# Stick-breaking attention handled two heads at a time, with split keys padded by zeros

## The chip, the cores and the metric

The kernel runs on one core of a Trainium2 chip, as one launch. The metric is the device time of that launch in microseconds; lower is better. The core has a matrix engine (TensorE, PE in the profile, with its weight loads as PEld), three engines for elementwise work (VectorE = DVE, ScalarE = ACT, GpSimd = POOL) and a queue for transfers (SyncE = SP). Each engine runs its own instructions in the order written and waits on the others through semaphores. Products of matrices end in PSUM banks of 128 x 512 float32.

## The reference

Two decoder blocks over 256 tokens of width 1024, in float32: first stick-breaking attention (12 heads of 64) beside softmax attention into 256 memory tokens, and a squared-relu feed-forward; then latent attention, a long convolution, and a convolutional feed-forward after each. The change touches the stick-breaking attention alone:

```
for blk in range(seq // 128):                       # two blocks of 128 queries
    t0 = blk * 128; t1 = t0 + 128
    z = einsum('bhtd,bhsd->bhts', q[t0:t1], k[:t1]) * 64 ** -0.5
    strict = arange(t1)[None, :] < arange(t0, t1)[:, None]
    log_stay = where(strict, log_sigmoid(-z), 0.0)
    later = cumsum(log_stay, axis=3, reverse=True) - log_stay
    w = where(strict, exp(log_sigmoid(z) + later), 0.0)
    out[t0:t1] = einsum('bhts,bhsd->bhtd', w, v[:t1])
```

So the weight of key s for query t is sigmoid(z[t, s]) times the product of sigmoid(-z[t, j]) over the keys j between s and t; keys at or after t count nothing.

## The kernel before

Every weight matrix comes from HBM in slabs of 128 x 1024 float32 (`weights`, L80). A slab is split into a high part on ACT (`whi`, L69) and a low part on DVE (`wlo`, L70), both in fp32r. A product is then three passes: high x high, low x high, high x low (`gemm_b`, `mm3`); the trace has one matmul record for such a pass and two for a product in plain float32. Raw slabs have a ring of 3 buffers, split ones a ring of 5, so SP can issue a slab's transfer only when the slab three places earlier has been split.

Stick-breaking attention comes second in the program, after the product for the values (`v_sb`). The 12 heads are 6 pairs, because one 128-row projection holds two heads of 64. `u_q(i)` and `u_k(i)` project the queries and keys of pair i: 24 matmuls of 256 columns each (L102) and one copy from PSUM on ACT (L351). The loop `pipeline` takes one head per turn: `scores` of the next head, then a filler (a projection for a later pair, or work of the memory attention), then `turn` of this head, then `values` of the head before.

- `scores` (L387 to L403) takes a head's 64 rows of q and k in plain float32: queries 0 to 127 against keys 0 to 128 (L391, 129 columns) and queries 128 to 255 against all keys (L393, 256 columns). After each, a bf16 product of the identity with a mask adds -1e30 where a key may not count (L392, L394). ACT takes sigmoid(-z/8) into `sb_stay` (L397) and sigmoid(z/8) into `sb_w` (L398), 385 columns each; DVE forms the running product from the right, `sb_later` (L400, a scan; `reset` starts it again at 1 between the two blocks), and multiplies `sb_w` by it (L402).
- `turn` transposes the weights on PE (L408, three 128 x 128 tiles into bank `wt`) and copies them back (L410).
- `values` multiplies by v in plain float32 (L418, L419) into half of the rows of bank `pv`; after the second head of a pair the result is split (`mix`).

The z banks of the two heads of a pair are two (`z00`, `z01`); the first sigmoid in the program needs another activation table (ACT_TABLE_LOAD).

The order on each engine is settled when the program is built: a scheduler places the instructions of these functions by its own model of their times.

Of the kernel before, what the change touches and what calls it, by code (L numbers as in the profile page):

```python
# [9 lines left out]
F32 = mybir.dt.float32  # L10
# [35 lines left out]
def block_kernel(ctx, tc, A, out, taps=None):  # L46
# [25 lines left out]
    # The splits of the slabs that follow a norm queue behind it on the vector engine.  # L72
# [7 lines left out]
    def weights(ap, dst=None):  # L80
        """Loads a slab of weights and splits it; where the vector engine is short, GpSimd shares the work."""
# [13 lines left out]
    def gemm_b(ps, w, off, x, kts):  # L95
        """ps[n, tok] = W[:, n-tile]^T x^T, x feature-major as (hi, lo)."""
# [29 lines left out]
    def range_reduce(dst, src, n, shift):  # L126
        """dst = src - 2 pi round(src / 2 pi + shift), kept inside the interval that Sin takes."""
# [50 lines left out]
    def first_mm(b, x, ws, utok):  # L178
        """The next product's first 512 columns for one token block, token-major."""
# [13 lines left out]
    def first_pair(utok, i, ps=None):  # L193
        """Two of the four first n-tiles, feature-major."""
# [55 lines left out]
    def spare(pool, tags):  # L250
        """Room outside the ring for the next product's first slabs: two of them for each pair of tags."""
# [45 lines left out]
    # ================= stick-breaking attention and memory attention =================  # L297
# [10 lines left out]
    # Products of zeros bring the tensor engine's clock up while the first loads are under way.  # L308
# [24 lines left out]
    identb = p1.tile([P, P], BF16, name="identb")  # L333
    nc.vector.tensor_copy(identb, ident)
    maskf = p1.tile([P, P + 1], F32, name="maskf")
    nc.sync.dma_start(maskf, A["c_mask"])
    maskb = p1.tile([P, P + 1], BF16, name="maskb")
    nc.vector.tensor_copy(maskb, maskf)
    reset = p1.tile([P, 385], F32, name="reset")
    nc.vector.memset(reset, 0.0)  # L340
    nc.vector.memset(reset[:, 128:129], 1.0)
    memx = (p1.tile([P, KT, S], F32R, name="mh"), p1.tile([P, KT, S], F32R, name="ml"))
# [10 lines left out]

    def u_q(i):
        proj(f"q_{i}", A["w_qk"][i], x, 3)

    def u_k(i):
        proj(f"k_{i}", A["w_qk"][6 + i], x, 3)
# [22 lines left out]
    class Stick:  # L381
        pv = None

        def __init__(self, head):
            self.h, self.pair, self.hh = head, head // 2, head % 2
# [26 lines left out]
        def values(self):  # L412
            if self.hh == 0:
                Stick.pv = acc_bank(1, 1, "pv")
# [764 lines left out]
```

## Time and profile before

| | us |
|---|---|
| median of three runs | 1000.65 (1000.11 to 1004.74) |
| span of the profiled execution | 1001.1 |
| PE busy in it | 963.8 (96%) |
| DVE, ACT, POOL busy | 752.7 (75%), 522.3 (52%), 123.5 (12%) |
| chain that ended last, share of PE | 76% |

The span runs from the first to the last instruction of one execution. PE counts as busy while a matmul is in it; matmuls overlap, so the time that one takes of a stream is read from starts, or from the chain of work that ended last, which follows the program back from its end and gives each piece only the time by which it held up the next. Stick-breaking attention lies between 32 and 114 us of the span; its last four heads share that time with the memory attention.

### The profile page before, as it was taken

The page shows a single profiled execution, that of the slowest core. Times are in us where ns is not written, and L with a number is a line of the kernel's source. Part 1 is how long each engine was busy: PE and PEld are TensorE (multiplying, and loading weights), DVE is VectorE, ACT ScalarE, POOL GpSimd, SP SyncE. Part 2 cuts the span into 40 slices and gives each one's busy share as a digit, 9 for nine tenths or more (in the row PEclk, how much of TensorE's full clock was granted, in tenths as well). Part 3 has the DMA queues.
Part 4 walks back from the last instruction along what each step waited for, and adds up shares of the span by engine and source line. Part 5 has one row for each costly group of instructions (what it writes and reads, how often), then busy time and mean ns, then how long its engine had stood idle before and what let it go on. Part 6 is the DMA issues. An engine that isn't in the chain of part 4 may idle for free.

```text
span 1001.1 us, 15605 instructions
## 1 busy us (share of the span) xinstructions
PE 963.8 (96%) x6056; PEld 849.8 (85%) x6056; DVE 752.7 (75%) x1158; ACT 522.3 (52%) x853; POOL 123.5 (12%) x78
## 2 busy tenths in 40 slices
PE   9999999999999999999999999998888899999996
PEld 7787878988988888788899999788787689999995
DVE  5565577766656778778979888859999778777776
ACT  4555545544445476546656566344354346555551
POOL 0000000000000110002231211166642100000000
PEclk9899999999999999999999999999998899999999
DMA  7742346666666462546555556443332555555551
GB/s 247 267 148 85 127 127 220 191 185 174 186 190 199 143 180 85 189 154 236 188 192 188 171 176 193 153 135 116 108 104 84 168 169 188 183 182 185 189 190 42
DMA packets 49065, 166.04 MB, mean 166 GB/s; under 512 B 6011, under 2 KB 7004, under 8 KB 48864
## 3 DMA queue, kind: packets, MB, share of 16 engines
q1 hardware_dynamic: 48800, 164.40, 50.4%
q8 instruction: 47, 0.77, 0.3%
q0 software_dynamic: 192, 0.66, 0.3%
q14 instruction: 26, 0.21, 0.1%
HBM read 163.33 MB, written 1.05 MB: 164 GB/s over the span
## 4 chain that ended last, share of the span: by engine, by line
PE 76%; DVE 12%; DMA 5%; ACT 3%; issue 3%; POOL 1%; SPq 0%; DVEq 0%; ACTq 0%; POOLq 0%
PE up L102 29%; PE acc L107 8%; PE acc L108 8%; PE acc L109 8%; PE f L189 5%; PE proj L102 4%; DVE wlo L70 2%; ACT whi L69 1%; DMA wraw<-w_v 1%; DVE yl L70 1%; DVE spec_q L939 1%; DVE spec_q L938 1%; DMA wraw<-hy_w_in 1%; PE qn L102 1%; PE z L107 1%
## 5 line engine op out<-in xcount | busy, mean ns | idle before, releaser
L70 DVE TENSOR_TENSOR wlo<-wraw,whi 128x1024 fp32r<-128x1024 f32 (+1 forms) x246 | 300.1, 1223 | 86.3 <-ACT whi L69 85.7
L69 ACT ACTIVATE whi<-wraw 128x1024 fp32r<-128x1024 f32 (+1 forms) x270 | 280.9, 1044 | 111.6 <-PE acc L108 52.8
L102 PE MATMUL up<-xh,whi 128*128 128x256 f32 x864 | 122.0, 283 | 1.6 <-DVE t L746 1.6
L102 PEld LDWEIGHTS up<-xh,whi 128*128 128x128 f32 x864 | 115.3, 191 | 8.6 <-ACT whi L69 2.3
L102 PE MATMUL up<-xh,wlo 128*128 128x256 f32 x864 | 121.3, 283 | 0.0
L102 PE MATMUL up<-xl,whi 128*128 128x256 f32 x864 | 121.2, 283 | 0.0
L108 PE MATMUL acc<-whi,hl 128*128 128x512 f32 x304 | 119.6, 394 | 0.6 <-DVE hl L70 0.6
L109 PE MATMUL acc<-wlo,hh 128*128 128x512 f32 x304 | 119.6, 395 | 0.0
L107 PE MATMUL acc<-whi,hh 128*128 128x512 f32 x304 | 119.3, 393 | 0.0
L102 PEld LDWEIGHTS up<-xl,whi 128*128 128x128 f32 x864 | 111.4, 192 | 0.0
L102 PEld LDWEIGHTS up<-xh,wlo 128*128 128x128 f32 x864 | 111.4, 192 | 0.0
L156 POOL TENSOR_TENSOR ln_rs<-ln_rs,mhalf 128x1 f32<-128x1 f32 x12 | 11.7, 971 | 642.2 <-DVE ln_rs L155 642.2
L743 ACT ACTIVATE t<-up,wc 128x256 f32<-128x256 f32 x80 | 37.7, 473 | 94.5 <-PE up L102 94.3
L744 DVE SCALAR_TENSOR_TENSOR t<-up,wc,t 128x255 f32<-128x255 f32 x80 | 38.2, 479 | 51.4 <-ACT t L743 51.4
L109 PEld LDWEIGHTS acc<-wlo,hh 128*128 128x128 f32 x304 | 57.1, 188 | 12.7
L108 PEld LDWEIGHTS acc<-whi,hl 128*128 128x128 f32 x304 | 57.1, 188 | 12.0 <-DVE hl L70 1.6
L107 PEld LDWEIGHTS acc<-whi,hh 128*128 128x128 f32 x304 | 57.6, 189 | 10.9 <-ACT hh L69 0.5
L70 POOL TENSOR_TENSOR wlo<-wraw,whi 128x1024 fp32r<-128x1024 f32 x24 | 59.7, 2504 | 55.9 <-ACT whi L69 55.9
L746 DVE SCALAR_TENSOR_TENSOR t<-up,wc,t 128x255 f32<-128x255 f32 x80 | 38.3, 480 | 2.1
L507 ACT ACTIVATE h<-up 128x256 f32<-128x256 f32 x28 | 10.8, 384 | 54.4 <-PE up L102 52.2
L508 DVE TENSOR_TENSOR h<-h 128x256 f32<-128x256 f32 x32 | 13.5, 424 | 26.7 <-ACT h L507 26.2
L812 POOL TENSOR_TENSOR Kf<-f_eo 128x512 f32<-128x512 f32 x16 | 23.1, 1464 | 63.3 <-ACT f_eo L809 63.3
(409 smaller groups left out, 1702.9 us busy)
## 6 DMA issues: line engine op xcount, KB each, us to landing
wraw<-ffn_w_up SPq DMA_DIRECT2D x80, 512.0 KB, 4.1
wraw<-ffn_w_down SPq DMA_DIRECT2D x44, 512.0 KB, 3.3
wraw<-w_down SPq DMA_DIRECT2D x32, 512.0 KB, 3.6
wraw<-w_up SPq DMA_DIRECT2D x28, 512.0 KB, 3.6
wraw<-hy_w_in SPq DMA_DIRECT2D x20, 512.0 KB, 3.3
wraw<-w_qk SPq DMA_DIRECT2D x14, 512.0 KB, 4.3
wraw<-w_out SPq DMA_DIRECT2D x8, 512.0 KB, 3.4
wraw<-mla_w_o SPq DMA_DIRECT2D x8, 512.0 KB, 3.2
```

Source lines behind the costliest of these rows:

```text
L69: nc.scalar.activation(hi, src, AF.Copy)
L70: eng.tensor_tensor(lo, src, hi.bitcast(F32), op=ALU.subtract)
L102: nc.tensor.matmul(ps, a[:, off + k * P:off + (k + 1) * P], m[:, k, :], start=i == 0, stop=i == len(seq) - 1)
L107: nc.tensor.matmul(ps, ah, mh, start=start, stop=False)
L108: nc.tensor.matmul(ps, al, mh, start=False, stop=False)
L109: nc.tensor.matmul(ps, ah, ml, start=False, stop=stop)
L189: nc.tensor.matmul(ps, x[xi][:, k, tb], ws[k // 2][wi][:, o:o + 512], start=i == 0, stop=i == len(seq) - 1)
L508: nc.vector.tensor_tensor(h, h, h, op=ALU.mult)
L743: norm["act"] = nc.scalar.activation(dst, ps, AF.Copy, scale=w3[:, 1:2])
L744: nc.vector.scalar_tensor_tensor(dst[:, 1:], ps[:, :S - 1], w3[:, 0:1], dst[:, 1:], op0=ALU.mult, op1=ALU.add)
L746: norm["dve"] = nc.vector.scalar_tensor_tensor(dst[:, :S - 1], ps[:, 1:S], w3[:, 2:3], dst[:, :S - 1], op0=ALU.mult, op1=ALU.add)
L812: nc.gpsimd.tensor_tensor(Kf[:, o, i, j, cs], eo[0], eo[1], op=op)
```

## The change

Keys of a pair are kept in split form and padded: for each pair there are a high and a low tile of 128 rows x 2 x 256 columns, where head 0 has its 64 rows filled in the first half and zeros below, and head 1 zeros above and its rows in the second half. The zeros are written once at the start. Queries are split as they are. A product of a pair's queries with such a tile, over all 128 rows, gives the scores of both heads side by side: three fp32r passes of 256 columns for the first block of queries (bank `z01`, "early") and three of 512 for the second ("late", bank `z00`). No mask is added; the scan now starts from 0 and is lifted to 1 at a query's own key by the identity laid into `reset`, which makes the weights of the keys at or after it zero. One scan (774 columns) and one product (768) do a pair; sigmoids are four for a pair, of 256, 256, 512 and 512 columns; the transposes are six into two banks. The loop has a turn for each pair, and its fillers are the two projections of a pair. The tiles for the memory tokens take the place of two that the next layer's first slabs use later.

```diff
-    reset = p1.tile([P, 385], F32, name="reset")
+    reset = p1.tile([P, 2, 3, 129], F32, name="reset")
     nc.vector.memset(reset, 0.0)
-    nc.vector.memset(reset[:, 128:129], 1.0)
-    memx = (p1.tile([P, KT, S], F32R, name="mh"), p1.tile([P, KT, S], F32R, name="ml"))
+    for hh in range(2):
+        for g in (0, 2):
+            nc.vector.tensor_copy(reset[:, hh, g, :P], ident)
+    stays = [p1.tile([P, 2, 3, 129], F32, name=f"sb_stay{i}") for i in range(2)]
+    for t in stays:
+        nc.vector.memset(t[:, :, :, P:], 0.0)
+        nc.vector.memset(t[:, :, 1, P:], 1.0)
+
+    keys = [[p1.tile([P, 2, S], F32R, name=f"k{t}{i}") for t in "hl"] for i in range(2)]
+    for ts in keys:
+        for t in ts:
+            nc.vector.memset(t[64:, 0, :].bitcast(F32), 0.0)
+            nc.vector.memset(t[:64, 1, :].bitcast(F32), 0.0)
+    memx = [p1.tile([P, KT, S], F32R, name=t, tag=t) for t in F4_TAGS[0]]
...
     def u_q(i):
-        proj(f"q_{i}", A["w_qk"][i], x, 3)
+        qk["q", i] = act_split(p1, proj_mm(A["w_qk"][i]), "sbq", 3)
 
     def u_k(i):
-        proj(f"k_{i}", A["w_qk"][6 + i], x, 3)
+        ps = proj_mm(A["w_qk"][6 + i])
+        kh, kl = keys[i % 2]
+        for hh in range(2):
+            r = slice(64 * hh, 64 * hh + 64)
+            split(kh[r, hh, :], kl[r, hh, :], ps[r])
...
         def scores(self):
-            r = slice(64 * self.hh, 64 * self.hh + 64)
-            q, k = qk[f"q_{self.pair}"], qk[f"k_{self.pair}"]
-            z = acc_bank(0, self.hh, "z")
-            nc.tensor.matmul(z[:, 0:129], q[r, 0:P], k[r, 0:129], start=True, stop=False)
-            nc.tensor.matmul(z[:, 0:129], identb, maskb, start=False, stop=True)
-            nc.tensor.matmul(z[:, 129:385], q[r, P:S], k[r, :], start=True, stop=False)
-            nc.tensor.matmul(z[:, 257:385], identb, maskb[:, :P], start=False, stop=True)
...
+            q, k = qk["q", self.pair], keys[self.pair % 2]
+            late, early = acc_bank(0, 0, "z"), acc_bank(0, 1, "z")
+            mm3(early[:, :S], [t[:, :P] for t in q], [t[:, :, :P] for t in k], True, True)
+            mm3(late, [t[:, P:] for t in q], [t for t in k], True, True)
+            ze = early[:, :S].rearrange("p (h s) -> p h s", h=2)
+            zl = late.rearrange("p (h g s) -> p h g s", h=2, g=2)
+            stay = stays[self.pair % 2]
+            w = p1.tile([P, 2, 3, P], F32, name="sb_w", tag="sb_w", bufs=2)
+            for t, sc in ((stay, -0.125), (w, 0.125)):
+                nc.scalar.activation(t[:, :, 0, :P], ze, AF.Sigmoid, scale=sc)
+                nc.scalar.activation(t[:, :, 1:, :P], zl, AF.Sigmoid, scale=sc)
+            later = p1.tile([P, 2, 3, 129], F32, name="sb_later", tag="sb_later", bufs=2)
+            flat = [t.rearrange("p h g s -> p (h g s)")[:, ::-1] for t in (later, stay, reset)]
+            nc.vector.tensor_tensor_scan(flat[0], flat[1], flat[2], 0.0, op0=ALU.mult, op1=ALU.max)
+            nc.vector.tensor_tensor(w, w, later[:, :, :, 1:], op=ALU.mult)
             self.w = w
...
         def values(self):
...
+            o = acc_bank(1, 1, "pv")
+            for b in range(2):
+                for hh in range(2):
+                    c = slice((2 * self.pair + hh) * 64, (2 * self.pair + hh) * 64 + 64)
+                    r = slice(64 * hh, 64 * hh + 64)
+                    nc.tensor.matmul(o[r, b * P:S], v_sb[:, b, c], self.wt[b][:, hh, :],
+                                     start=b == 0, stop=b == 1)
...
-    u_q(0), u_k(0), u_q(1)
-    filler = {0: [(u_k, 1)], 8: [(u_k, 5), (u_mem,)], 9: [(u_km, 0)], 10: [(u_qm, 0)], 11: [(u_vm,)],
-              12: [(u_km, 1), (u_qm, 1)], 13: [(u_dn, 0)], 14: [(u_dn, 1), (u_dn, 2)], 15: [(u_dn, 3)]}
...
+    u_q(0), u_k(0), u_q(1), u_k(1)
+    filler = {p - 2: [(u_q, p), (u_k, p)] for p in range(2, SB_PAIRS)}
+    filler |= {4: [(u_mem,), (u_km, 0), (u_qm, 0)], 5: [(u_vm,)], 6: [(u_km, 1), (u_qm, 1)],
+               7: [(u_dn, 0)], 8: [(u_dn, 1), (u_dn, 2)], 9: [(u_dn, 3)]}
```

Three places show the new order. The first is ACT at the start of the attention, around the first sigmoids. Before (`q_1`, `k_1` are copies of the second pair's projections; `whi_579`, `whi_633`, `whi_690` are the slabs of q of pair 3, k of pair 3 and q of pair 4; z00 and z01 are heads 0 and 1):

```order
L69 ACTIVATE whi_579<-wraw_578 128x1024
L351 ACTIVATE q_1_390<-proj_365 128x256
L397 ACT_TABLE_LOAD
L397 ACTIVATE sb_stay_398<-z00_392 128x385
L398 ACTIVATE sb_w_397<-z00_392 128x385
L397 ACTIVATE sb_stay_410<-z01_404 128x385
L398 ACTIVATE sb_w_409<-z01_404 128x385
L69 ACTIVATE whi_633<-wraw_632 128x1024
L351 ACTIVATE k_1_447<-proj_422 128x256
L69 ACTIVATE whi_690<-wraw_689 128x1024
L410 ACTIVATE sb_wt_453<-wt10_449 128x384
```

The same place in the change (`kh1` is the high tile of the keys of pair 1, written in two halves; `whi_579`, `whi_614` and `whi_686` are the slabs of q and k of pair 3 and of q of pair 4; z01_449 and z00_448 belong to pair 0, z01_465 to pair 1):

```order
L69 ACTIVATE whi_579<-wraw_578 128x1024
L69 ACTIVATE sbqh_409<-proj_384 128x256
L69 ACTIVATE whi_614<-wraw_613 128x1024
L69 ACTIVATE kh1_295<-proj_419 64x256
L416 ACT_TABLE_LOAD
L416 ACTIVATE sb_stay0_287<-z01_449 128x2x128
L416 ACTIVATE sb_w_456<-z01_449 128x2x128
L417 ACTIVATE sb_stay0_287<-z00_448 128x2x2x128
L417 ACTIVATE sb_w_456<-z00_448 128x2x256
L69 ACTIVATE kh1_295<-proj_419 64x256
L69 ACTIVATE whi_686<-wraw_685 128x1024
L416 ACTIVATE sb_stay1_288<-z01_465 128x2x128
```

The split of the slab for k of pair 3 has moved ahead of the table load and the first sigmoids, and the second half of `kh1` stands behind them. The second place is PE at the same time. Before (proj_422 is k of pair 1, proj_473 q of pair 2):

```order
L393 MATMUL z01_404<-k_0_357,q_0_324 128x256
L394 LDWEIGHTS identb_281
L394 MATMUL z01_404<-maskb_285,identb_281 128x128
L102 MATMUL proj_422<-xh_87,whi_417 128x256 x8
L102 MATMUL proj_422<-xh_87,wlo_418 128x256 x8
L102 MATMUL proj_422<-xl_88,whi_417 128x256 x8
L408 MATMUL wt10_449<-ident_79,sb_w_397 128x128 x3
L102 MATMUL proj_473<-xh_87,whi_468 128x256
L391 MATMUL z00_455<-k_1_447,q_1_390 128x129
```

In the change (proj_419 is k of pair 1, proj_486 q of pair 2; z with 449 and 448 is pair 0, with 465 and 464 pair 1):

```order
L102 MATMUL proj_419<-xl_88,whi_414 128x256 x8
L107 MATMUL z01_449<-kh0_293,sbqh_339 128x256
L108 MATMUL z01_449<-kh0_293,sbql_340 128x256
L109 MATMUL z01_449<-kl0_294,sbqh_339 128x256
L107 MATMUL z00_448<-kh0_293,sbqh_339 128x512
L108 MATMUL z00_448<-kh0_293,sbql_340 128x512
L109 MATMUL z00_448<-kl0_294,sbqh_339 128x512
L102 MATMUL proj_486<-xh_87,whi_481 128x256 x8
L102 MATMUL proj_486<-xh_87,wlo_482 128x256 x5
L107 MATMUL z01_465<-kh1_295,sbqh_409 128x256
L108 MATMUL z01_465<-kh1_295,sbql_410 128x256
L107 MATMUL z00_464<-kh1_295,sbqh_409 128x512
```

The projection of k of pair 1 now precedes the first scores, and between the scores of pair 0 and of pair 1 stand 13 matmuls of the next projection; the first transposes follow only after two more projections. The third place is PE in the middle of the attention, one turn of the loop. Before, one head (turn of head 3, values of head 2, scores of head 5):

```order
L408 MATMUL wt10_665<-ident_79,sb_w_571 128x128 x3
L418 MATMUL pv11_617<-sb_wt_615,v_sb_107 64x256
L419 MATMUL pv11_617<-sb_wt_615,v_sb_107 64x128
L102 MATMUL proj_695<-xh_87,whi_690 128x256
L391 MATMUL z00_677<-k_3_663,q_3_609 128x129
L392 LDWEIGHTS identb_281
L392 MATMUL z00_677<-maskb_285,identb_281 128x129
L393 MATMUL z00_677<-k_3_663,q_3_609 128x256
L394 LDWEIGHTS identb_281
L394 MATMUL z00_677<-maskb_285,identb_281 128x128
L102 MATMUL proj_695<-xh_87,whi_690 128x256 x7
```

In the change, one pair:

```order
L428 MATMUL wt10_648<-ident_79,sb_w_472 128x128 x2
L428 MATMUL wt1_649<-ident_79,sb_w_472 128x128
L428 MATMUL wt10_648<-ident_79,sb_w_472 128x128 x2
L428 MATMUL wt1_649<-ident_79,sb_w_472 128x128
L439 MATMUL pv11_660<-sb_wt256_558,v_sb_107 64x256 x2
L439 MATMUL pv11_660<-sb_wt128_559,v_sb_107 64x128 x2
L102 MATMUL proj_691<-xh_87,whi_686 128x256 x4
L107 MATMUL z01_670<-kh1_295,sbqh_609 128x256
L108 MATMUL z01_670<-kh1_295,sbql_610 128x256
L107 MATMUL z00_669<-kh1_295,sbqh_609 128x512
L108 MATMUL z00_669<-kh1_295,sbql_610 128x512
L102 MATMUL proj_691<-xh_87,whi_686 128x256 x2
```

Six transposes and four products with v (two heads next to each other, each into its own half of the rows of `pv`) now come between the end of a key projection and the scores that use it.

## Rows read from the trace of the kernel before

**Rows 1.** Busy time by stretch; columns: each engine, granted clock, DMA share, GB/s.

```profile
37.70:39.70 2.00, 0.03 (x1) 0.00 (x0) 2.00 (x4) 2.00 (x6) 0.00 (x0) 1.00 1.04 412
...
40.50:47.30 6.80, 6.80 (x29) 5.81 (x29) 3.40 (x4) 1.42 (x4) 0.00 (x0) 0.50 1.01 357
...
52.80:113.80 61.00, 61.00 (x422) 50.33 (x421) 35.16 (x48) 33.62 (x66) 0.00 (x0) 1.00 0.38 121
```

**Rows 2.** Chain of work that ended last, 74.9 to 86 us: start, us, what.

```profile
74.94 0.33 PE wt L408 x3
75.27 0.57 PE pv L418 x2
75.85 0.22 PE pv L419 x2
76.07 0.31 PE proj L102
76.38 0.42 PE z L391 x2
76.80 0.16 PE z L392
76.96 0.63 PE z L393 x2
77.58 0.16 PE z L394
77.75 2.80 PE proj L102 x23
...
83.03 2.92 PE proj L102 x24
```

**Rows 3.** The same chain later: fp32r streams of 256 and of 512 columns.

```profile
107.16 5.91 PE proj L102 x48
...
116.02 0.23 PE acc L109
```

**Rows 4.** Timeline of ACT, 26 to 41 us: start, us, line, what [idle before].

```profile
27.48 1.06 ACT L69 ACTIVATE whi<-wraw 128x1024 fp32r<-128x1024 f32 x1 [1.09 <-DMA wraw<-w_qk]
28.44 0.37 ACT L351 ACTIVATE q<-proj 128x256 f32<-128x256 f32 x1
...
34.21 1.06 ACT L69 ACTIVATE whi<-wraw 128x1024 fp32r<-128x1024 f32 x1 [0.75 <-DMA wraw<-w_qk]
...
35.56 1.28 ACT L397 ACT_TABLE_LOAD   x1
36.86 0.49 ACT L397 ACTIVATE sb_stay<-z 128x385 f32<-128x385 f32 x1
37.24 0.49 ACT L398 ACTIVATE sb_w<-z 128x385 f32<-128x385 f32 x1
```

**Rows 5.** Timeline of PE, 24 to 41 us.

```profile
25.19 1.12 PE L102 MATMUL proj<-xl,whi 128*128 128x256 f32 x8
...
36.61 1.12 PE L102 MATMUL proj<-xl,whi 128*128 128x256 f32 x8
39.74 0.52 PE L408 MATMUL wt<-ident,sb_w 128*128 128x128 f32 x3 [2.01 <-ACT k L351]
```

**Rows 6.** A slab's transfer in the chain, 14 to 50 us.

```profile
29.82 4.31 DMA wraw<-w_qk
```

**Rows 7.** Timeline of SP: the issue of the slab for k of pair 3.

```profile
32.31 0.33 SPq L87 DMA_DIRECT2D wraw<-w_qk  x1
```

**Rows 8.** Groups by line and form, 40 to 114 us: count, busy us, mean ns.

```profile
L70 DVE TENSOR_TENSOR wlo<-wraw,whi 128x1024 fp32r<-128x1024 f32 x15 | 18.2, 1223 | 16.6 <-ACT whi L69 16.6
...
L400 DVE TENSOR_TENSOR_SCAN sb_later<-sb_stay,reset 128x384 f32<-128x384 f32 x10 | 9.6, 956 | 9.1 <-ACT sb_stay L397 9.1
...
L402 DVE TENSOR_TENSOR sb_w<-sb_w,sb_later 128x384 f32<-128x384 f32 x11 | 6.1, 558 | 1.2
...
L351 ACT ACTIVATE k<-proj 128x256 f32<-128x256 f32 x4 | 1.5, 384 | 6.2 <-PE proj L102 6.2
```

More of the change, by code (lines that the diff above doesn't have):

```diff
@@ L352, in proj, with proj_mm @@
         qk[name] = t
+    def proj_mm(wap):
+        w = weights(wap)
+        ps = bank("proj")
+        gemm_b(ps[:, :S], w, 0, x, KT)
+        return ps[:, :S]
     def u_q(i):
-        proj(f"q_{i}", A["w_qk"][i], x, 3)
+        qk["q", i] = act_split(p1, proj_mm(A["w_qk"][i]), "sbq", 3)
     def u_k(i):
-        proj(f"k_{i}", A["w_qk"][6 + i], x, 3)
+        ps = proj_mm(A["w_qk"][6 + i])
[3 more added lines that the diff above has]
+            split(kh[r, hh, :], kl[r, hh, :], ps[r])
     def u_qm(i):
@@ L381, in block_kernel, with __init__ @@
     class Stick:
[L382 to L385 removed]
+        def __init__(self, pair):
+            self.pair = pair
         def scores(self):
[L388 to L402 removed]
@@ L403, in scores @@
+            nc.vector.tensor_tensor(w, w, later[:, :, :, 1:], op=ALU.mult)
             self.w = w
         def turn(self):
-            tps = acc_bank(1, 0, "wt")
-            for i, o in enumerate((0, 129, 257)):
-                nc.tensor.transpose(tps[:, i * P:(i + 1) * P], self.w[:, o:o + P], ident)
-            self.wt = p1.tile([P, 384], F32, name="sb_wt", tag="sb_wt", bufs=2)
-            nc.scalar.activation(self.wt, tps[:, :384], AF.Copy)
-        def values(self):
-            if self.hh == 0:
-                Stick.pv = acc_bank(1, 1, "pv")
-            o = Stick.pv
-            c = slice(self.h * 64, self.h * 64 + 64)
-            r = slice(64 * self.hh, 64 * self.hh + 64)
-            nc.tensor.matmul(o[r, :S], v_sb[:, 0, c], self.wt[:, :S], start=True, stop=False)
-            nc.tensor.matmul(o[r, P:S], v_sb[:, 1, c], self.wt[:, S:], start=False, stop=True)
-            if self.hh == 1:
-                mix[self.pair] = act_split(p1, o[:, :S], f"mix{self.pair}", 1)
+            first, second = acc_bank(1, 0, "wt"), bank("wt1")
@@ new lines, in turn @@
+            for hh in range(2):
+                for g, ps, c in ((0, first, 2 * hh), (1, first, 2 * hh + 1), (2, second, hh)):
+                    nc.tensor.transpose(ps[:, c * P:(c + 1) * P], self.w[:, hh, g, :], ident)
+            self.wt = [p1.tile([P, 2, n], F32, name=f"sb_wt{n}", tag=f"sb_wt{n}", bufs=2) for n in (S, P)]
+            for t, ps, n in zip(self.wt, (first, second), (2 * S, S)):
+                nc.scalar.activation(t, ps[:, :n].rearrange("p (h t) -> p h t", h=2), AF.Copy)
@@ new lines, in values @@
+        def values(self):
+            o = acc_bank(1, 1, "pv")
+            for b in range(2):
+                for hh in range(2):
+                    c = slice((2 * self.pair + hh) * 64, (2 * self.pair + hh) * 64 + 64)
+                    r = slice(64 * hh, 64 * hh + 64)
+                    nc.tensor.matmul(o[r, b * P:S], v_sb[:, b, c], self.wt[b][:, hh, :],
+                                     start=b == 0, stop=b == 1)
+            mix[self.pair] = act_split(p1, o[:, :S], f"mix{self.pair}", 1)
@@ L481, in u_late @@
             gb.extend(ln_load(p1, A["ln_mix_g"], A["ln_mix_b"]))
-    filler[5].append((u_late,))
-    pipeline([Stick(h) for h in range(12)] + [Mem(h) for h in range(4)], filler)
+    filler[2].append((u_late,))
+    pipeline([Stick(p) for p in range(SB_PAIRS)] + [Mem(h) for h in range(4)], filler)
     for k in range(4, 8):
@@ L1091, in _shape_constants @@
     c["c_ident"] = np.eye(P, dtype=f32)
-    t, s = np.arange(P)[:, None], np.arange(P + 1)[None, :]
-    c["c_mask"] = np.where(s >= t, f32(-1e30), f32(0.0)).astype(f32)
     tt, ff = np.arange(S)[:, None], np.arange(S)[None, :]
```

18 lines of the change are left out of this document (removed).

## The prediction

> **What bounds the kernel now.** I first read the busy times by stretch, to see what the matrix engine does while the attention runs. From 52.8 to 113.8 us it is busy in every microsecond at the full clock (granted 1.00, 2.4 GHz), while DVE works 35.2 and ACT 33.6 of the 61 us and the transfer engines 0.38 of the time [rows 1]. So there a microsecond less of matmuls is a microsecond less of time, as long as nothing that PE needs comes late.
>
> Next the chain of work that ended last, which gives the pace of one turn: it goes from PE to PE without another engine in between. Two heads, one pair, take 5.60 us (wt 0.33, pv 0.57 + 0.22, proj 0.31 + 2.80, z 0.42 + 0.16 + 0.63 + 0.16) and 5.41 us (the same, with the projection in one piece of 2.92), together 11.01 us [rows 2]. The scores are 1.37 us of each head.
>
> The start is different. PE stands still for 2.0 us, from 37.7 to 39.7, with ACT and DVE busy all that time, and then the granted clock is 0.50 (1.2 GHz) from 40.5 to 47.3 us [rows 1], so that 6.8 us do the work of 3.4. The two timelines say why it stood: the transposes of the first head waited [rows 5] for ACT's table load of 1.28 us, two sigmoids and a scan behind it [rows 4]. ACT's queue also shows work held up by a slab: the copy of q_0 began at 28.44, although its matmuls, the last of which are the eight from 25.19 on, had ended at about 26.3 [rows 5]; the slab split ahead of it had waited 1.09 us for its transfer [rows 4].
>
> **The change part by part, in the steady turns.** Scores of a pair before: 2 x 1.37 = 2.74 us. After: three passes of 256 and three of 512 columns. A stream of 256-column passes goes at 5.91 / 48 = 0.12 us each, a 512-column pass takes 0.23 [rows 3]: 3 x 0.12 + 3 x 0.23 = 1.06 us. The rows with zeros cost nothing extra there, since those streams use all 128 rows too. Projections: 48 matmuls x 0.118 = 5.7 us. They took 0.31 + 2.80 + 2.92 = 6.03 because a first pass behind plain float32 or bf16 work costs up to 0.19 more (0.31 against 0.12) [rows 2]; now only one such change per pair is left, behind pv: 5.69 + 0.19 = 5.88. Transposes (2 x 0.33) and products with v (2 x 0.79) keep their matmuls, 2.25 us. A pair: 1.06 + 5.88 + 2.25 = 9.2 us, which is 1.8 less than 11.0, six times, 10.9 us. If the first passes of early and late each cost 0.19 more, because their operands have just been written, the gain of a pair is 1.43, 8.6 in all. I take 1.8: they stand in a running stream of the same kind, as the projection's own passes do.
>
> Work on the other engines, all beside PE: ACT has one more instruction of about 0.38 for each pair, since the keys' copy becomes two of 64 rows (as long as one of 128 rows at most, 384 ns [rows 8]); sigmoids and the copies of the transposes keep their columns (1536 against 1540, 768 against 768). DVE gets three subtractions of 256 columns, each no more than 0.56 (the 384-column product), and loses little: a scan of 774 columns instead of two of 384 lies between 0.96 and 2 x 0.956 = 1.9 us, and I take 1.9; the product of 768 columns lies between 0.56 and the 1.22 of a 1024-column split [rows 8]. DVE works 6.3 us of a pair's 11.0 now (35.2 / 61 of the time), ACT 6.1 (33.6 / 61) [rows 1]; with at most 1.7 and 0.4 us more they have 8.0 and 6.5 of 9.2, so neither becomes the bound.
>
> What must come in time: the scores of the next pair now use keys split directly before. Between the end of the key projection and these scores PE has six transposes, four products with v and three to nine projection passes, 0.66 + 1.58 + 0.4 = 2.6 us or more. On ACT stand a half of the keys (0.38), the copies of the transposes (about 1) or one slab split (1.06 [rows 4]), and the other half (0.38), about 2 us; on DVE a slab split (1.22) and two subtractions fall into the same time, and only the third pass needs their result. So the wait is covered, by about half a microsecond; for pair 2 there is no product with v ahead, ten passes (1.2) stand in its place, and it may wait 0.1 us.
>
> **The start.** This is where I expect to lose. By the order of the changed program the second half of the keys of pair 1 is behind, on ACT: the slab split for k of pair 3, the first half, the table load and the four sigmoids of pair 0. That slab is issued at 32.31, when a raw buffer comes free [rows 7]; nothing before that point changes by more than some tenths (the zeros and the four copies into `reset` lie between the first splits on DVE). A slab takes 4.3 us [rows 6], so it is there at 36.6; split 1.06, to 37.7; half of the keys 0.38, to 38.0; table 1.28, to 39.3; sigmoids at the pace of the rows, 0.38 for 385 columns (36.86 to 37.24), so 1.5 for 1536, to 40.8; other half, to 41.2 [rows 4]. PE meanwhile: the fourth projection ended at about 37.6 [rows 5] with the scores of two heads, 2.74, ahead of it; in the new order it ends at 34.9. Scores of pair 0 to 36.0, thirteen passes to 37.5, then it waits until 41.2: 3.7 us instead of 2.0. The subtraction for the same half is behind the scan of pair 0 (from 40.4, 1.9 long) and done at 42.7; PE gets there at about 42.2 at the full clock, and at 1.2 GHz not before, so 0 to 0.5 more. Loss 1.7 to 2.2 us; I take 1.9. The granted clock falls as it does now, and I expect the same 3.4 us for it; the first transposes, which wait today, come after two more projections and find their input ready.
>
> **The sum.** -10.9 + 1.9 = -9.0 us. On the profiled execution's 1001.1 us that is 992.1; the median of the runs, 1000.65, is 0.4 below it, so 991.6. Nothing after the attention changes, and the chain that ends last runs through it, so the gain should reach the end.
>
> **The rivals.** (a) *The products with v overlap.* They now come two heads next to each other, each into its own 64 rows of the bank. Before they were two products of the same head, and no row shows neighbours in different halves, so from rows the gain is between 0 and one head's 0.79 us for each pair [rows 2], 0 to 4.7 us: down to 986.9, or 989.2 for half of it. I count nothing for it in the sum, as every 64-column product in the rows runs after the one before. The Trainium skill, TensorEngine Tiling (Array Packing), Key Properties, speaks for it: different tiles can execute weight loads and matmuls in parallel. No run here shows it yet.
>
> (b) *The start costs more.* If the clock stays at 1.2 GHz in proportion to the idle time (3.7 against 2.0, so 12.6 us instead of 6.8), that is 2.9 us more; with the dearer first passes (+2.3) the gain shrinks to 3.8: 996.9. For it: the longer idle time. Against it: 6.8 us of slow clock came with work that was dense from 39.7 on, so idle time alone doesn't set it.
>
> (c) *Slower: every pair waits for its keys.* On ACT the halves of the keys stand behind slab splits, and a slab that is not there holds them up, as it held up q_0. It decides once a slab lands more than 2.6 us after the end of the key projection. One such stop of 2.0 us brought 3.4 us of slow clock with it [rows 1], 5.4 together; three of the four later pairs would cost 16 us, and the kernel would end at 1000.65 - 9.0 + 16.2 = 1007.9. Against it: the transfer engines have 0.38 of their time in use there, so slabs come early.
>
> **How the numbers follow.** The forecast, a gain of about 6 to 11.5 us, gets 0.66; (a) with a gain above that 0.16; (b) 0.13; (c) 0.05. The predicted time is that of the forecast, 991.6. The range runs from 986.5 (10.9 with no longer wait at the start and half of the overlap, 2.4, is 987.4; all of the overlap with the wait 986.9) to 996 (near (b)). Half a per cent, 5 us, is about what a measurement can tell from no change. Faster by more: the forecast and (a), 0.82; within it: (b), 0.13; slower: (c), 0.05.
>
> **What would show it.** In the changed kernel's chain a middle pair should take 9.2 us from the first transpose to the next pair's, with scores of 1.06; pv should be 1.58 for a pair, or near 1.1 or below under (a). PE should idle about 3.7 us from 37.5, ended by ACT's second half of `kh1`, and the clock be 0.50 for some 7 us after 40.5. The prediction is wrong if PE also idles ahead of the scores of pairs 3 to 5, if passes of 512 columns take more than 0.25, or if the clock falls again.

## The result and the profile after

The changed kernel takes 989.82 us (median of four runs, 988.23 to 991.58), the kernel before beside it 1000.38 (999.17 to 1004.74): a ratio of 0.988, 95% interval 0.985 to 0.991, 10.6 us less. The profiled execution took 988.41 us, its span is 986.6.

First the chain of work that ended last, over one middle pair of the changed kernel (start, us, what), to set against [rows 2]:

```profile
75.05 0.66 PE wt L428 x6
75.70 0.80 PE pv L439 x8
76.50 0.55 PE proj L102 x3
77.05 0.26 PE z L107
77.31 0.12 PE z L108
77.43 0.23 PE z L107
77.66 0.24 PE z L108
77.90 0.60 PE proj L102 x5
78.50 0.36 PE z L109 x2
78.86 4.76 PE proj L102 x40
83.62 0.66 PE wt L428 x6
```

From one first transpose to the next are 8.57 us, where two heads took 11.01. The transposes are as they were (0.66). The eight pv records of both heads take 0.80, and the four of one head took 0.79 [rows 2]: that is the surprise. The scores are 0.26 + 0.12 + 0.23 + 0.24 + 0.36 = 1.21, the projections 0.55 + 0.60 + 4.76 = 5.91. The dear one of the score passes is the first, 0.26 where a 256-column pass takes 0.12. The timelines of ACT and then of PE say why: the second half of its keys ended at 76.87, and the pass started right behind it, at 76.92.

```profile
76.49 0.38 ACT L69 ACTIVATE kh<-proj 64x256 fp32r<-64x256 f32 x1
```

```profile
76.92 0.39 PE L107 MATMUL z<-kh,sbqh 128*128 128x256 f32 x1
```

Then busy time by stretch (columns as in [rows 1]), and all that PE waited for between 23 and 105 us (us in total, times, longest):

```profile
38.10:40.50 2.40, 0.03 (x1) 0.00 (x1) 1.22 (x2) 2.34 (x7) 0.00 (x0) 0.91 0.97 377
40.07:43.48 3.41, 2.98 (x11) 2.69 (x12) 3.35 (x4) 2.05 (x4) 0.00 (x0) 0.50 0.99 314
68.80:100.40 31.60, 31.58 (x247) 28.83 (x248) 21.35 (x32) 19.35 (x40) 0.00 (x0) 1.00 0.44 146
```

```profile
PE z L107 <- ACT kh L69: 4.4, 3, 2.4
```

PE still stands once at the start, 2.4 us, and the clock is 0.50 (1.2 GHz) for 3.41 us instead of 6.8. The wait has another cause than before: scores now wait for the second half of the keys. Of the three waits, the other two are ahead of the scores of pairs 3 and 4. ACT's timeline shows what stood ahead of that half at the start (compare [rows 4]), PE's what waited and that the first transposes, for which PE stood in [rows 5], no longer wait:

```profile
35.77 1.06 ACT L69 ACTIVATE whi<-wraw 128x1024 fp32r<-128x1024 f32 x1 [1.36 <-DMA wraw<-w_qk]
36.73 0.36 ACT L69 ACTIVATE kh<-proj 64x256 fp32r<-64x256 f32 x1
37.11 1.28 ACT L416 ACT_TABLE_LOAD   x1
38.41 0.39 ACT L416 ACTIVATE sb_stay<-z 128x256 f32<-128x256 f32 x1
...
39.43 0.62 ACT L417 ACTIVATE sb_w<-z 128x512 f32<-128x512 f32 x1
40.07 0.38 ACT L69 ACTIVATE kh<-proj 64x256 fp32r<-64x256 f32 x1
...
57.33 0.38 ACT L69 ACTIVATE kh<-proj 64x256 fp32r<-64x256 f32 x1 [0.75 <-DVE kl L70]
```

```profile
40.50 0.58 PE L107 MATMUL z<-kh,sbqh 128*128 128x256 f32 x1 [2.37 <-ACT kh L69]
...
47.18 0.82 PE L428 MATMUL wt<-ident,sb_w 128*128 128x128 f32 x6
```

It is the queue that the prediction had read off the order: slab split, a half of the keys, table load, four sigmoids, the other half. In pairs 3 and 4 there is one thing more, which the last ACT row (pair 3) shows: the copy of the second half waits for DVE's subtraction of the first, and that stands behind two slab splits.

The slab for the keys of pair 3 ([rows 6] and [rows 7] before), and DVE's groups between 40 and 100 us ([rows 8]):

```profile
32.20 3.49 DMA wraw<-w_qk
```

```profile
L420 DVE TENSOR_TENSOR_SCAN sb_later<-sb_stay,reset 128x774 f32<-128x774 f32 x6 | 10.6, 1770 | 4.9 <-ACT sb_stay L417 4.9
L421 DVE TENSOR_TENSOR sb_w<-sb_w,sb_later 128x768 f32<-128x768 f32 x6 | 5.7, 955 | 0.4
```

A scan of a pair is 1.77, the product 0.96, both inside their bounds.

**How runs are compared below.** Executions of one kernel differ by several us, and with the mean granted clock: 23 of the kernel before lie between 997.1 us (clock 0.986) and 1006.6 (0.982). Much of that arises long after the attention, in stretches of half clock between 630 and 805 us whose number varies (in the profiles they cost 11.9 us before, 10.2 in the changed kernel, 15.3 in e3). So each kernel is also measured by two things that this does not touch: the start of the first `up` matmul, the first product behind the attention and its output product, in the profiled execution; and the mean over its executions of time x granted clock, which counts time as if at the full clock. The first rows of that matmul, before and after (count, duration min/median/max, first and last start):

```profile
L102 PE MATMUL up<-xh,whi x144: 277/283/384, 158.8 to 256.0; 128*128 128x256 f32 x144
```

```profile
L102 PE MATMUL up<-xh,whi x168: 277/283/384, 145.6 to 259.8; 128*128 128x256 f32 x168
```

So 13.2 us are gained by then, 1.7 of them from half clock at the start. The last table of this section has all kernels: one middle pair, what PE waited for in the attention, what half clock cost ahead of `up` (half the length of the stretch), the first `up`, the median of the runs and its ratio to before with its interval, and time x clock less that of the kernel before in the same comparison (standard error 0.5 to 1.2). One execution of e7, the profiled one, ran at a granted clock of 0.556 from end to end and took 1511.9 us; the median and the ratio leave it out, and its profile is not used for durations.

| kernel | pair | waits | half clock | `up` | median | ratio | time x clock |
|---|---|---|---|---|---|---|---|
| before | 11.01 | 2.0 | 3.4 | 158.8 | 1000.4 | 1 | 0 |
| changed | 8.57 | 4.4 | 1.7 | 145.6 | 989.8 | 0.988 (0.985 to 0.991) | |
| e1 pv by head | 8.58 | 4.9 | 0 | 144.7 | 992.9 | 0.991 (0.988 to 0.993) | -12.4 |
| e2 old, pv of a pair | 10.00 | 0.8 | 0 | 148.0 | 996.6 | 0.995 (0.992 to 0.997) | -5.8 |
| e3 old, no mask | 10.26 | 3.5 | 1.7 | 153.0 | 1001.9 | 1.000 (0.997 to 1.002) | -2.6 |
| e4 unpadded | 8.24 | 6.2 | 5.1 | 147.1 | 993.3 | 0.992 (0.989 to 0.994) | -11.9 |
| e5 projections first | 8.40 | 0.4 | 0 | 138.2 | 985.7 | 0.984 (0.982 to 0.987) | -13.7 |
| e6 the same, unpadded | 8.39 | 1.5 | 0 | 139.3 | 987.0 | 0.986 (0.983 to 0.989) | -14.8 |
| e7 the same, plain | | | | | 984.8 | 0.983 (0.981 to 0.986) | -16.0 |
| e8 pv apart | 9.34 | 4.0 | 1.7 | 150.2 | 996.4 | 0.993 (0.990 to 0.996) | -7.4 |
| e9 as e7, table early | 8.40 | 0.7 | 0 | 138.3 | 983.1 | 0.983 (0.979 to 0.986) | -17.7 |
| e10 table early | 8.58 | 3.1 | 1.7 | 144.5 | 990.0 | 0.989 (0.985 to 0.994) | -13.0 |
| e11 changed again | 8.57 | 5.2 | 1.7 | 145.7 | 993.1 | 0.990 (0.987 to 0.994) | -12.2 |
| e12 as e5 | 8.40 | 0.4 | 0 | 138.7 | 987.3 | 0.986 (0.982 to 0.990) | -13.7 |

The first three columns explain the fourth. Six times the difference of a pair, plus the difference of the waits, plus that of half clock gives -13.9 for the changed kernel (`up` moved by -13.2), -15.1 for e1 (-14.1), -10.7 for e2 (-10.8), -4.7 for e3 (-5.8), -10.7 for e4 (-11.7), -20.7 for e5 (-20.6), -9.7 for e8 (-8.6): right to about 1 us each time, and as near in the rows left out here. Time x clock has no half clock in it, so it is to be set against `up` without that column: -13.2 + 1.7 = -11.5 for the changed kernel, where e11 has -12.2. That agrees to 1.7 us in every row but e5 and e12, which keep 3.5 and 3.0 us less at the end than at `up`.

### The profile page after: what moved, and what is told of

It is laid out like the page before. It is cut to its first block, busy times and chain, and to the rows that moved or that the text cites. A ratio compares the mean times of both kernels' runs of the same rounds, so it can differ in the third digit from the quotient of the medians.

```text
span 986.6 us, 15543 instructions
## 1 busy us (share of the span) xinstructions
PE 946.4 (96%) x6020; PEld 841.1 (85%) x6020; DVE 760.4 (77%) x1177; ACT 524.5 (53%) x859; POOL 123.3 (12%) x78
## 4 chain that ended last, share of the span: by engine, by line
PE 76%; DVE 13%; DMA 5%; ACT 3%; issue 2%; POOL 0%; SPq 0%; DVEq 0%; ACTq 0%
PE up L102 30%; PE acc L108 8%; PE acc L107 8%; PE acc L109 8%; PE f L189 5%; PE proj L102 2%; DVE wlo L70 2%; PE z L107 1%; DMA wraw<-w_qk 1%; DVE yl L70 1%; DVE spec_q L956 1%; ACT whi L69 1%; DVE spec_q L955 1%; PE qn L102 1%; DMA wraw<-w_v 1%
## 5 line engine op out<-in xcount | busy, mean ns | idle before, releaser
L156 POOL TENSOR_TENSOR ln_rs<-ln_rs,mhalf 128x1 f32<-128x1 f32 x12 | 11.7, 971 | 629.1 <-DVE ln_rs L155 629.1
L107 PEld LDWEIGHTS acc<-whi,hh 128*128 128x128 f32 x304 | 57.6, 189 | 10.9 <-ACT hh L69 0.6
L524 ACT ACTIVATE h<-up 128x256 f32<-128x256 f32 x28 | 10.8, 385 | 54.7 <-PE up L102 51.5
```

The lines of the kernel that those rows point to most:

```text
L107: nc.tensor.matmul(ps, ah, mh, start=start, stop=False)
```

## The experiments

Theory 1: the gain is matmul time taken out of every pair, by cheaper scores and by two heads' products with v running at the same time; the keys' second half and the start give some of it back. The rivals are in the expectations.

**e1_pv_by_head.** The products with v in the old order.

```diff
-            for b in range(2):
-                for hh in range(2):
+            for hh in range(2):
+                for b in range(2):
```

> The changed kernel with the four products with v of a pair in the old order: both of one head, then both of the other, so that neighbours write the same 64 rows. Same products, same operands. Theory 1 (neighbours in different halves of the rows run at the same time, worth 0.8 us a pair): pv goes back from 0.80 to about 1.58 us a pair, the first `up` matmul from 145.6 to about 150.3 us, the kernel from 989.8 to about 994.5. Rival (the shorter pv comes from something else, as the operands' layout or records that are missing): pv stays at 0.80 in the chain and the time within 1 us of 989.8.

Its chain, pv of a middle pair:

```profile
74.75 0.81 PE pv L439 x8
```

pv stayed at 0.81, and by time x clock the kernel is the changed one (-12.4, e11 -12.2); the median, 992.9, lies between the two expectations. The single records show that the written order did change and what the engine makes of it: the second head's first record starts 13 to 15 ns behind the first head's in all six pairs, 6 to 7 ns in the changed kernel, while the next record of the same head starts some 270 ns later. Theory 1 as put (neighbours must be in different halves) is wrong. Two things were left: the halves run side by side in whatever order the two heads' products are written, or the cheaper pv has nothing to do with halves. e2 and e8 were to tell.

**e2_old_pv_pair.** In the kernel before, both heads' products with v after the second head's transposes (and a third buffer for the transposed weights).

```diff
+            if self.hh == 0:
+                Stick.first = self
+                return
+            o = acc_bank(1, 1, "pv")
+            for b in range(2):
+                for hd in (Stick.first, self):
+                    c = slice(hd.h * 64, hd.h * 64 + 64)
+                    r = slice(64 * hd.hh, 64 * hd.hh + 64)
+                    wt = hd.wt[:, S:] if b else hd.wt[:, :S]
+                    nc.tensor.matmul(o[r, b * P:S], v_sb[:, b, c], wt, start=b == 0, stop=b == 1)
...
```

> The kernel before with one thing of the change alone: the products with v of the two heads of a pair next to each other, half by half, after the second head's transposes. Theory 1: pv from 1.58 to 0.80 us a pair, 4.7 us less in all, 995.7 instead of 1000.4, and a little more where a stream's first pass is saved. Rival (the gain needs the new scores or one turn for a pair): 1.58 us a pair and 1000.4.

One pair in its chain:

```profile
72.82 0.33 PE wt L408 x3
...
77.76 0.80 PE pv L422 x8
...
82.82 0.22 PE wt L408 x2
```

pv is 0.80 for both heads, and the pair 10.00 instead of 11.01. This one part of the change is worth 5.8 us by time x clock, 5.7 by the medians. (Its `up` of 148.0 also has a shorter wait and no half clock in that execution, the fastest of its twelve.)

**e3_no_mask.** The kernel before with the two mask products of each head gone.

```diff
-            nc.tensor.matmul(z[:, 0:129], identb, maskb, start=False, stop=True)
...
-            nc.tensor.matmul(z[:, 257:385], identb, maskb[:, :P], start=False, stop=True)
```

> The kernel before without its 24 mask matmuls; it leaves out the causal mask, so the weights are not those of the reference. Theory 1 (the scores' gain of 1.5 us a pair is mostly that of one pass at full rate in place of plain float32): the two records of 0.16 us go, 0.64 us a pair, 3.8 us in all, 996.6. Rival (most of it was the switch between kinds of matmul that the mask brought): z of a pair falls from 2.74 to 1.3 us or less, 8 us or more in all, 992 or less.

One head and the projection behind it:

```profile
77.08 0.42 PE z L391 x2
77.50 0.43 PE z L392 x2
77.93 3.07 PE proj L102 x24
81.00 0.33 PE wt L406 x3
```

A head's scores fell from 1.37 to 0.85: the masks' own 0.32, and 0.20 in the 256-column product (0.63 to 0.43). But the projections behind got dearer (3.07 + 0.31 + 2.94 = 6.32 a pair instead of 6.03), so the pair gains 0.75. For the scores, 1.70 a pair lies halfway between what the two theories said; for the whole, 4.5 us, it is near theory 1. The kernel as a whole gained nothing, though: `up` came 5.8 us earlier, but the mean granted clock over its twelve executions is 0.9812 against 0.9836, which is 2.4 us, and time x clock shows 2.6 us gained. Why these executions had more half clock behind the attention stays open.

**e4_unpadded.** Keys split but not padded, heads in turn.

```diff
...
+            passes = ((0, 0), (1, 0), (0, 1))
+            for t, zc, kc in ((slice(0, P), slice(0, P), slice(0, P)), (slice(P, S), slice(P, 3 * P), slice(0, S))):
+                for n, (a, m) in enumerate(passes):
+                    for hh in range(2):
+                        r = slice(64 * hh, 64 * hh + 64)
+                        nc.tensor.matmul(z[hh][:, zc], q[a][r, t], k[m][r, kc], start=n == 0, stop=n == 2)
...
```

> The changed kernel with keys not padded: the split keys of both heads in one 128-row tile (one copy on ACT, one subtraction on DVE instead of two and two), each head's scores from its own 64 rows into a bank of its own, passes of the two heads in turn, 128 and 256 columns. Theory 1 carried on (halves of the rows can run at the same time too): z of a pair from about 1.2 to 0.6 to 0.7 us; and since the keys no longer go from ACT to DVE and back, PE's wait at the start falls from 2.37 us to under 0.5, and the waits ahead of pair 3 (0.5) and pair 4 (1.5) shrink: 982 to 985 in all. Rival A (halves of the rows run one after the other): z stays at 1.1 to 1.3 us, only the waits shrink, 985 to 987. Rival B (the single pass at full rate needs all 128 rows): z grows to 2 us or more, and the time is that of the changed kernel or longer.

The scores of a middle pair in its chain, and PE's wait at the start in its timeline:

```profile
78.37 0.88 PE z L405 x12
```

```profile
42.21 0.47 PE L405 MATMUL z<-sbkh,sbqh 64*128 64x128 f32 x1 [5.30 <-ACT sb_w L411]
```

z is 0.88, between the theory's 0.6 to 0.7 and rival A's 1.1. The gain of a pair (8.24) is buried: the scores of pair 1 were placed right behind the first projection passes and waited 5.3 us for the sigmoids of pair 0, which read the same banks, and half clock then cost 5.1. I had expected that wait under 0.5 us.

**e5_projections_first.** The changed kernel with a turn's projections ahead of the next pair's scores, in the stick-breaking turns only.

```diff
-            if i + 1 < len(heads):
+            stick = i + 1 < len(heads) and isinstance(heads[i + 1], Stick)
+            if not stick and i + 1 < len(heads):
                 heads[i + 1].scores()
             for f, *a in filler.get(i, []):
                 f(*a)
+            if stick:
+                heads[i + 1].scores()
             hd.turn()
```

> The changed kernel with one thing moved: in each turn of the stick-breaking heads the two projections of the turn are written ahead of the next pair's scores instead of behind them, so that a pair's keys have a whole turn (5.8 us of projections) before they are read. Theory (what is left of the loss is waits for the keys' second half on ACT, 4.4 us, and the 1.7 us of work that half clock cost behind the first of them): PE no longer waits for kh, the clock stays at full level at 40 us, and the first `up` matmul falls from 145.6 to 139.5 us (138.5 to 140.5), the kernel from 989.8 to about 984. Rival (ACT and DVE are late as such, so that the wait only moves to the first transposes or to a later pair): as much idle time at another line, `up` stays at 144 to 146.

A pair in its chain:

```profile
67.78 0.66 PE wt L428 x6
...
69.24 5.90 PE proj L102 x48
75.14 0.12 PE z L107
...
75.96 0.23 PE z L109
76.18 0.66 PE wt L428 x6
```

The waits are gone but for 0.4 us, and with them half clock at the start; `up` comes 7.4 us ahead of the changed kernel's, at 138.2, a little earlier than expected; the median is 985.7, not 984. Unbroken, and with their keys there a turn ahead, the scores take 76.18 - 75.14 = 1.04 us, which is the 1.06 that the prediction had from [rows 3].

**e6_projections_first_unpadded.** e4's scores in e5's order.

> The unpadded scores of e4_unpadded with the projections ahead of the next pair's scores as in e5_projections_first. Theory: e4's gain of 0.3 us a pair in z (0.88 against about 1.2) was hidden by its wait of 5.3 us at the start, which came from the order (pair 1's scores behind pair 0's sigmoids, which reuse their banks) and goes now: z 0.88, the first `up` matmul 1 to 2 us ahead of that of e5_projections_first, about 138 us. Rival (the 5.3 us come from unpadded keys as such): PE waits 3 us or more at the start again and `up` is at 142 us or later.

Transposes and scores of a pair in its chain:

```profile
68.76 0.81 PE wt L422 x6
...
76.26 0.89 PE z L405 x12
```

The 5.3 us are gone, so they came from the order; 1.5 us of waiting for the first pair's weights took their place. In the pair nothing is won: z is 0.15 shorter than in e5, and the transposes, which now come right behind scores of 64 rows, are 0.15 longer (0.81). `up` is 1.1 us behind e5's where I had said 1 to 2 ahead.

**e7_plain_side_by_side.** As e6, with queries and keys in plain float32.

```diff
...
+            for t, zc, kc in ((slice(0, P), slice(0, P), slice(0, P)), (slice(P, S), slice(P, 3 * P), slice(0, S))):
+                for hh in range(2):
+                    r = slice(64 * hh, 64 * hh + 64)
+                    nc.tensor.matmul(z[hh][:, zc], q[r, t], k[r, kc], start=True, stop=True)
...
```

> As e6_projections_first_unpadded, but queries and keys stay plain float32 as in the kernel before (one copy each on ACT, no split, no subtraction on DVE): four score matmuls of a pair instead of twelve, the two heads next to each other in their own 64 rows, without mask matmuls (the scan and the rest are the changed kernel's). Theory 1 carried on (what cost time before was one head at a time and the mask, not plain float32 as such): z of a pair 0.8 to 0.95 us, as with the split, `up` within 1 us of that of e6. Rival (single passes at full rate are what made the scores cheap): 1.5 to 1.7 us a pair, as two heads without mask cost in e3_no_mask (2 x 0.85), `up` 4 to 5 us later than in e6.

By time it is level with e6 or ahead (984.8 against 987.0); the cost of z was left to e9.

**e8_pv_apart.** The first head's products with v ahead of the transposes, the second's behind.

```diff
...
+            if i and isinstance(heads[i - 1], Stick):
+                heads[i - 1].values(0)
             hd.turn()
-            if i:
+            if i and isinstance(heads[i - 1], Stick):
+                heads[i - 1].values(1)
+            elif i:
                 heads[i - 1].values()
```

> The changed kernel with the products with v of the two heads of a pair apart: the first head's ahead of the six transposes, the second head's behind them. Same products. Theory (the heads' products run at the same time as long as nothing else stands between them, in whichever order, as e1_pv_by_head showed): pv goes back to 2 x 0.79 us = 1.58 a pair instead of 0.80, and a middle pair takes 0.8 us more, 4.7 us in six pairs. Rival (the shorter pv has another cause, such as the layout of the transposed weights): the two pieces add up to 0.8 to 0.9 us, and the time is that of the changed kernel.

The same place in its chain:

```profile
76.00 0.80 PE pv L441 x4
76.79 0.80 PE wt L428 x6
77.60 0.80 PE pv L441 x4
```

pv is back at 0.80 + 0.80, and `up` 4.6 us later than in the changed kernel. With e1 and e2 this settles it: products into different halves of the rows run at the same time when nothing else stands between them, in whichever order they are written.

**e9_plain_first_table.** e7 with a sigmoid of one column at the very start.

> As e7_plain_side_by_side, with one sigmoid of a single column added at the very start, so that ACT's sigmoid table is loaded while the first transfers run. It gives z of plain float32 side by side at the full clock, which the profile of e7 (clock 0.556 all the way) could not show. Theory 1 carried on: z 0.8 to 0.95 us a pair, transposes 0.81 (as behind the unpadded scores of e6), a pair 8.3 to 8.5 us, the first `up` matmul within 1 us of e6's 139.3 or, if PE's wait of 1.5 us ahead of the first transposes there was for the table, 1.3 us earlier. Rival (single passes at full rate matter for the scores): z 1.5 us or more, a pair 9.1 or more, `up` later than 142.

Scores and transposes in its chain:

```profile
75.32 0.86 PE z L405 x8
76.18 0.81 PE wt L422 x6
```

Plain float32 side by side costs 0.86, no more than the split passes side by side (0.89, e6). Two heads one after the other without mask cost 1.70 (e3). So for heads side by side the rival falls: there the split into single passes saves nothing.

For the scores of the changed kernel this is not shown. Its padded tiles don't use the two halves side by side; they send the columns of both heads through all rows, one head's behind the other's, and no run has such tiles in plain float32. An estimate: e3's 256 columns in plain float32 took 0.43, so 768 would take 1.29, against 1.04 for the passes (e5). Of the 0.66 between 1.70 and 1.04, then, some 0.25 may be the single passes, and the other 0.4 that the products of both heads run as one (129 columns took 0.42 in e3, twice a pair, where that pace makes it 0.22).

PE's wait for the first transposes fell from 1.5 to 0.7. At 983.1 us this is the shortest of all, though its ratio is no better than e7's (0.983 both).

**e10_table_early.** The changed kernel with that early sigmoid alone.

```diff
+    early = const.tile([P, 1], F32, name="early")
+    nc.scalar.activation(early, ones, AF.Sigmoid)
```

> The changed kernel with one sigmoid of a single column added at the very start, nothing else. Theory (PE's wait at the start is ACT's chain of slab split, half of the keys, table load, four sigmoids, other half): without the 1.28 us of the table load the wait falls from 2.37 to about 1.1 us, the first `up` matmul from 145.6 to 144.3, and to 142.6 if the clock then stays at its full level. Rival (another input, the slab or DVE, ends the wait): 2.2 us or more of waiting, `up` 145 to 146.

The wait and, in ACT's timeline, the slab split that begins the queue:

```profile
39.74 0.39 PE L107 MATMUL z<-kh,sbqh 128*128 128x256 f32 x1 [1.94 <-ACT kh L69]
```

```profile
36.46 1.06 ACT L69 ACTIVATE whi<-wraw 128x1024 fp32r<-128x1024 f32 x1 [0.78 <-DMA wraw<-w_qk]
```

The wait is 1.94 instead of 1.1: the slab was split 0.7 us later than in the changed kernel's profile (36.46 against 35.77), which ate half of the 1.28. 2.37 - 1.28 + 0.69 is 1.8. The table is one link of the queue and the slab another; half clock came all the same. `up` is at 144.5, 1.1 us earlier.

**e11_changed_again and e12_projections_first_again**, the changed kernel and e5 on one chip.

> The changed kernel itself, on the same chip as e12: a pair 8.6 us, the first `up` matmul at 145 to 146 us, 0.985 to 0.991 of the kernel before.

> e5_projections_first on the same chip as the changed kernel itself: a pair 8.4 us, the first `up` matmul 7 us ahead of e11's (138 to 139), and the whole kernel 4 to 7 us shorter than e11's.

`up` at 145.7 and 138.7, the whole kernel 993.1 and 987.3: 5.8 us apart. Time x clock differs by 1.6 only (errors of 1.1 each), which does not tell the two apart. Of the 7 us at `up`, 1.7 are half clock, and a part of the other 5.3 is given back behind `up`: the eleven largest groups of PE's waits from 130 us to the end add up to 30.8 us in e12 and 28.6 in e5, against 27.5 in e11, 25.9 in the changed kernel's first profile and 25.6 in e9. The largest single difference is one of the norms, PE's wait for `xt`, in e11 and then in e12:

```profile
PE ln_t L169 <- DVE xt L161: 1.9, 2, 1.4
```

```profile
PE ln_t L169 <- DVE xt L161: 4.3, 2, 3.7
```

What makes DVE late there in e12 was not tried. The rest of the 5.8 is the clock (0.985 on average against 0.982); whether the order of the turns brings that about was not tried either. e9, with the same order of turns, keeps more: 5.5 us less than e11 by time x clock.

## Why the prediction was right, and where it was not

The time lies in the range, 1.8 us below the 991.6, and the main step holds: the matmuls of the attention bound the time, and less of them in a pair is less time. The sum's terms were not all right.

- **Scores, 2.74 to 1.06 a pair.** Measured 1.21. The 512-column passes took 0.23 to 0.24, as taken from [rows 3], so the rows of zeros cost nothing; the first pass took 0.26 because its keys came just ahead of it. That is the dearer case that the prediction weighed and did not take (operands just written), for one pass of the two. In e5, where the keys are there a turn earlier, the scores take 1.04. Masks gone are worth 0.75 of a pair (e3). What of the rest is single passes and what is both heads in one product was only estimated (e9). Neither splitting nor padding was needed for it: plain float32 with the heads side by side takes 0.86.
- **Projections 5.88, transposes 0.66.** Measured 5.91 and 0.66.
- **Products with v, 1.58 a pair: this step failed.** They cost 0.80, six times 0.8 is 4.7 us, and this was rival (a), to which the prediction gave 0.16. No row of before had both heads next to each other, and the value taken was the end of the bound that changes nothing. The Trainium skill, TensorEngine Tiling (Array Packing), Key Properties, had it right: different tiles can execute in parallel. The runs agree, with eight records in 0.80 us where four took 0.79, and show that the order among them does not matter (e1).
- **Pair 9.2.** Measured 8.57, so 14.6 us in six pairs instead of 10.9.
- **DVE and ACT do not become the bound.** Right: between 68.8 and 100.4 us PE is busy in all but 0.02, DVE 21.4, ACT 19.4 of 31.6.
- **The keys' wait is covered by half a microsecond: failed.** Pairs 3 and 4 waited 0.5 and 1.5 us. The estimate counted the work between on each engine, but not that the second copy on ACT waits for the first subtraction on DVE, nor that splits of the memory slabs would stand in front. It cost 2.0 us in the changed kernel, 1.9 in e11. The prediction had named idle time ahead of the scores of pairs 3 to 5 as a sign of being wrong. It is a small piece of rival (c), though the slab splits that held up the second half stood on DVE, not on ACT.
- **PE waits 3.7 us at the start, ended by ACT's second half.** The mechanism is right, the size was 2.37: the slab took 3.49 us instead of 4.31, and PE came 0.6 later. In e11 and e1 the same wait was 3.27 and 2.92, so the estimate was off by less than one execution suggests. One reading of the kernel before was off here: [rows 5] names ACT's copy of k_1 as what ended the old wait. It stands in ACT's queue behind the table load, all four sigmoids and a slab split, and ended at 39.71; the product behind the first head's scan, which the prediction named, had ended at 39.64.
- **Half clock costs 3.4 us as before.** It cost 1.7. In e5, with no wait, nothing.

The loss of waits, 2.4 us more than before, is near the 1.9 allowed, but only because a shorter wait at the start and two unforeseen ones added up. Pairs -14.6, waits +2.4, half clock -1.7 is -13.9; -13.2 was there at `up`. Without the half clock 11.5 are left at `up`, and time x clock, which has none in it, shows 12.2 at the end (e11, error 1.2): all of it reaches the end, where the forecast had 9.0. The medians show 10.6 in the first comparison and 7.6 in the second (e11: 1000.7 to 993.1), since executions of the changed kernel spread from 988.2 to 996.1 us with the half clock behind the attention. So that 989.8 lies 1.8 us from 991.6 is in part luck: the sum was about 3 us short, above all by pv, and a median of four executions can be off by as much.

e5 and e9 beat both kernels: 0.984 and 0.983 of before. Against the changed kernel on the same chip, e12 gains 5.8 us and e9, in the same comparison, 10.0 (983.1 against 993.1); by time x clock it is 1.6 and 5.5.

## What to carry to other kernels

Put products that use different halves of the rows or columns directly behind each other before you make each of them cheaper; the old kernel could have had 5.8 us (e2) by moving the four products of each pair together, with one more buffer. When a step is split into pieces that go between two engines, follow the chain from piece to piece (copy, subtraction, copy) and not the sum of work on each engine. And write the work that nothing waits for ahead of the work that has just lost its slack: moving the scores behind the projections (e5) took out all but 0.4 us of the 4.4 that the new scores had brought in waits, even if by time x clock little of that is left at the end (1.6 us, e12 against e11).

## What was not expected of the hardware

- The two halves work side by side also if both products of one half are written before those of the other (e1: 0.81; apart, e8: 1.60).
- Changing the shape costs time at the seam: six transposes took 0.66 behind 128-row work and 0.81 behind scores of 64 rows (e6, e9), 0.80 behind products with v (e8). The Trainium skill, TensorEngine Tiling (Array Packing), Key Properties, says that a change of the tiling mode drains the engine; the rows agree, and put it near 0.15 us here.
- The granted clock did not follow the wait at 40 us: after waits of 2.37, 3.27 and 1.94 (changed, e11, e10) half clock cost 1.7 each time, after waits of 3.5 (e3, e8) 1.7 as well, after one of 2.92 (e1) nothing, after one of 2.0 (before) 3.4, after one of 5.3 (e4) 5.1. PE's timeline in e1, and then in e11:

```profile
40.74 0.39 PE L107 MATMUL z<-kh,sbqh 128*128 128x256 f32 x1 [2.92 <-ACT kh L69]
```

```profile
40.66 0.58 PE L107 MATMUL z<-kh,sbqh 128*128 128x256 f32 x1 [3.27 <-ACT kh L69]
```

The same pass took 0.39 us at the full clock in e1 and 0.58 at half clock in e11.
